# A row-wise log-sum-exp on one core: the logs of the first 51 rows stored in fifteen small pieces between two loads

## The chip, the cores and the metric

The kernel runs on one core of a Trainium2 chip. The metric is the device time in microseconds (us) of one execution. Three runs of the kernel before gave 162.51, 162.53 and 162.57 us, a median of 162.53 us.

## What is computed

The input x is float32 of shape 32 x 512 x 1024; the reduction runs over the last axis, and the output is 32 x 512 float32.

```python
def reference(x, axis):
    x_max = np.max(x, axis=axis, keepdims=True)
    return (x_max.squeeze(axis) + np.log(np.sum(np.exp(x - x_max), axis=axis))).astype(np.float32)
```

The kernel first takes log(sum(exp(x))) without the maximum, in one pass over x, and checks that every sum lies between 1e-18 and 1e18. Only where one does not, a second pass with the maximum runs; with the data of the runs it is skipped.

## The kernel before

**Tiling.** The 16,384 rows of 1024 numbers are spread over 128 partitions, 128 rows to a partition (`x_v`, line 64). Below, "row t" means the t-th row of every partition, 4 KB in each of 128 partitions. The rows go through a ring of 51 row slots in SBUF (`ring`, line 75). `CHUNKS` (line 10) cuts the 128 rows into 17 loads of 4, 15, 16, 16, 16, 14, 13, 9, 7, 5, 4, 3, 2, 1, 1, 1 and 1 rows. They are called load 0 to load 16 here, and the rows of load i are chunk i. So loads 0 to 3 bring the first 51 rows, load 5 has 14 rows, load 6 has 13, load 7 has 9, load 10 has 4 and load 16 is the last row.

**Engines.** All loads and stores are issued by SyncE (SP) in program order, on one DMA queue. `load` (line 135) makes SP wait until VectorE (DVE) or ScalarE (ACT) has finished with the slots that the load overwrites, and then issues one DMA (line 155; line 146 for load 16). ACT takes the exponential of a chunk in place, in one or two pieces (line 235); DVE sums the pieces (line 255, or line 242 row by row). Some rows are summed by ACT itself (line 262, line 225), among them the last four, whose sums go to the PSUM tile `late`.

**Logs.** `take_logs` (line 157) makes ACT wait for the sums of a range of rows and write their logarithm to `res` (line 162). It is called three times: in the turn of chunk 7 (`LN_AT = 7`, line 217) for the 81 rows of chunks 0 to 5, in the turn of the last chunk (line 221) for 43 more rows, and at the end (line 272) for the last four.

**Stores and end.** After all loads, SP waits for the second logs and stores 124 columns of `res` (line 276), then waits for the third and stores the last 4 (line 278). A row of the output is 128 numbers, 512 B, for a partition. Meanwhile DVE compares the sums with the bounds (line 283), TensorE counts the votes (lines 304 and 307), DVE forms the verdict (line 312), and SP, DVE and ACT load it and branch (lines 316 to 321). SP then waits for the other two (line 347), clears the semaphores, and waits for both stores (line 348).

What sets the order around the change is therefore SP's list: a wait there holds back every load behind it.

Of the kernel before, what the change touches and what calls it, by code (L numbers as in the profile page):

```python
# [21 lines left out]
PARTS = ((0, 128, 2), (1, 128, 4), (3, 128, 8), (7, 64, 8), (71, 128, 8))  # L22


LN_AT = 7
LN_LAG = 1


LATE = 4
# [9 lines left out]
def kernel(  # L39
# [6 lines left out]
    nc = tc.nc  # L46
    P = nc.NUM_PARTITIONS
# [17 lines left out]
    out_v = bass.AP(tensor=out.tensor, offset=out.offset, ap=[[NB, P], [1, NB]])  # L65
# [11 lines left out]
    res = nc.alloc_sbuf_tensor("res", [P, NB], fp32).ap()  # L77
# [14 lines left out]
    act_done = nc.alloc_semaphore("act_done")  # L92
# [5 lines left out]
    again = nc.alloc_semaphore("again")  # L98
    act_again = nc.alloc_semaphore("act_again")
    dve_again = nc.alloc_semaphore("dve_again")  # L100
    stored = nc.alloc_semaphore("stored")
    used = sorted(
        sem.num
        for sem in [
            *landed,
            *(act_done, dve_done, pool_done, counted, judged, passed),
            *(again, act_again, dve_again),
        ]
    )
    assert used == list(range(used[0], used[0] + len(used)))  # L110
# [18 lines left out]
    acts = dves = 0  # L129

    def cuts(n, parts):
        ends = [-(-n * k // parts) for k in range(parts + 1)]
        return [(lo, hi) for lo, hi in zip(ends, ends[1:]) if lo < hi]

    def load(i):
        (s, row), r = place[i], CHUNKS[i][0]
        act_wait = max(a for a, _ in busy[s : s + r])
        dve_wait = max(d for _, d in busy[s : s + r])
        if dve_wait:
            nc.sync.wait_ge(dve_done, dve_wait)  # L140
        if act_wait:
            nc.sync.wait_ge(act_done, act_wait)
        dst, src = ring[:, s : s + r], x_v[:, row : row + r]
        if i == len(CHUNKS) - 1:
            for k, (lo, hi) in enumerate(spans):
                nc.sync.dma_start(out=dst[:, :, lo:hi], in_=src[:, :, lo:hi]).then_inc(
                    landed[i + k], 16
                )
        elif i in UNEVEN:
            for first, last, step in PARTS:  # L150
                nc.sync.dma_start(
                    out=dst[first:last:step], in_=src[first:last:step]
                ).then_inc(landed[i], 16)
        else:
            nc.sync.dma_start(out=dst, in_=src).then_inc(landed[i], 16)

    def take_logs(lo, hi, src, dve_wait, act_wait, bias=0.0):
        nonlocal acts
        nc.scalar.wait_ge(act_done, act_wait)
        if dve_wait:  # L160
            nc.scalar.wait_ge(dve_done, dve_wait)
        nc.scalar.activation(out=res[:, lo:hi], in_=src, func=Ln, bias=bias).then_inc(  # L162
            act_done, 1
        )
        acts += 1

    late_row = place[-LATE][1]
    assert not any(n_dve for _, n_dve, _, _ in CHUNKS[-LATE:])

    def total(t):  # L170
        return late[:, t - late_row : t - late_row + 1] if t >= late_row else sums[:, t : t + 1]
# [10 lines left out]
    def pieces(lo, hi):  # L182
        return [(lo + a, lo + b) for a, b in cuts(hi - lo, PIECES)]
# [5 lines left out]
    with nc.body("second_vector", valid_engines=vector):  # L189
        for k, (lo, hi) in enumerate(steps):  # L190
# [5 lines left out]
                out=part, in0=part, in1=peak[:, lo:hi].unsqueeze(2).to_broadcast([P, hi - lo, D])  # L196
# [14 lines left out]
    logged = 0  # L211
    done_before = [(0, 0)]
    for i, (r, n_dve, parts, by_halves) in enumerate(CHUNKS):
        if i:
            load(i)
        s, row = place[i]
        if i == LN_AT:
            logged = place[i - LN_LAG][1]
            take_logs(0, logged, sums[:, :logged], *done_before[i - LN_LAG])
        if i == len(CHUNKS) - 1:  # L220
            take_logs(logged, late_row, sums[:, logged:late_row], *done_before[-LATE])
            early_logs = acts
            for k, (lo, hi) in enumerate(spans):
                nc.scalar.wait_ge(landed[i + k], 16)
                nc.scalar.activation(  # L225
                    out=ring[:, s, lo:hi],
                    in_=ring[:, s, lo:hi],
                    func=Exp,
                    accum_out=late[:, LATE - 1 + k : LATE + k],
                ).then_inc(act_done, 1)  # L230
                acts += 1
            continue
        nc.scalar.wait_ge(landed[i], 16 * (len(PARTS) if i in UNEVEN else 1))
        for lo, hi in cuts(n_dve, parts):
            nc.scalar.activation(  # L235
                out=ring[:, s + lo : s + hi], in_=ring[:, s + lo : s + hi], func=Exp
            ).then_inc(act_done, 1)
            acts += 1
            nc.vector.wait_ge(act_done, acts)
            if by_halves:  # L240
                for j in range(lo, hi):
                    nc.vector.tensor_tensor_reduce(  # L242
                        out=ring[:, s + j, : D // 2],
                        in0=ring[:, s + j, : D // 2],
                        in1=ring[:, s + j, D // 2 :],
                        scale=1.0,
                        scalar=0.0,
                        op0=Alu.add,
                        op1=Alu.add,
                        accum_out=sums[:, row + j : row + j + 1],  # L250
                    ).then_inc(dve_done, 1)
                    dves += 1
                    busy[s + j] = (0, dves)
            else:
                nc.vector.reduce_sum(  # L255
                    out=sums[:, row + lo : row + hi], in_=ring[:, s + lo : s + hi], axis=AX
                ).then_inc(dve_done, 1)
                dves += 1
                for j in range(lo, hi):
                    busy[s + j] = (0, dves)  # L260
        for j in range(n_dve, r):
            nc.scalar.activation(  # L262
                out=ring[:, s + j],
                in_=ring[:, s + j],
                func=Exp,
                accum_out=total(row + j),
            ).then_inc(act_done, 1)
            acts += 1
            busy[s + j] = (acts, 0)
        done_before.append((dves, acts))  # L270
# [2 lines left out]


    nc.sync.wait_ge(act_done, early_logs)
    nc.sync.dma_start(out=out_v[:, :late_row], in_=res[:, :late_row]).then_inc(stored, 16)
    nc.sync.wait_ge(act_done, acts)
    nc.sync.dma_start(out=out_v[:, late_row:], in_=res[:, late_row:]).then_inc(stored, 16)

# [1 line left out]
    def compare(lo, hi, values):  # L281
# [13 lines left out]
        out=ends[:, 1:], in_=sums[:, :late_row], axis=AX, op=Alu.min  # L295
# [26 lines left out]
    with nc.body("second_pass", valid_engines=[*vector, *others]):  # L322
        for k, (lo, hi) in enumerate(steps):
            if k:
                nc.sync.wait_ge(dve_again, 3 * k)
            for a, b in pieces(lo, hi):
                nc.sync.dma_start(
                    out=ring[:, a - lo : b - lo], in_=x_v[:, a:b]
                ).then_inc(again, 16)
        nc.sync.wait_ge(dve_again, 3 * len(steps) + 1)  # L330
        nc.sync.wait_ge(stored, 32)
        nc.sync.dma_start(out=out_v, in_=res).then_inc(stored, 16)
        nc.sync.wait_ge(stored, 48)
        nc.sync.sem_inc(stored, -16)

        for k, (lo, hi) in enumerate(steps):
            part = ring[:, : hi - lo]
            nc.scalar.wait_ge(dve_again, 3 * k + 2)
            nc.scalar.activation(out=part, in_=part, func=Exp).then_inc(act_again, 1)
        nc.scalar.wait_ge(dve_again, 3 * len(steps))  # L340
        nc.scalar.wait_ge(stored, 32)
        nc.scalar.activation(out=res, in_=sums, func=Ln).then_inc(act_again, 1)
        nc.br("last", engines=[*vector, *others])
    nc.switch_bb("last", parent=opening)

    nc.sync.wait_ge(passed, 2)
    nc.sync.sem_clear(range(used[0], used[-1] + 1))
    nc.sync.wait_ge(stored, 32)
# [47 lines left out]
```

## Time and profile before

| | us |
|---|---|
| median of 3 runs | 162.53 |
| the profiled execution | 162.67 |
| its span, first to last instruction | 161.3 |
| around the span in that execution | 1.37 |
| busy in the span: DVE / ACT | 121.9 / 115.1 |
| DMA, share of 16 engines' span | 97.4% |
| DMA packets | 2737, of them 560 under 512 B |

The profile is one execution, recorded by the hardware. Its page gives the busy time of each engine, the DMA activity in 40 slices of the span, the chain of work that ended last, and groups of instructions by source line. The trace behind it also holds when each semaphore was raised by each DMA engine, and a record (start, duration, size) of each DMA packet.

### The profile page before, as it was taken

The numbers are of one execution on the slowest core, as the hardware profiler recorded it, in microseconds if no ns is written. First come the engines' busy times: TensorE is split into PE (matmuls) and PEld (weight loads), VectorE is DVE, ScalarE is ACT, GpSimd is POOL, SyncE is SP. The second block draws the span as 40 slices with busy tenths as digits, with TensorE's granted clock in tenths as the row PEclk, the third lists the DMA queues.
The fourth block names the chain that finished last, engine by engine and source line by source line (L and its number), as shares of the span: only waits on it lengthen the run. The fifth ranks groups of instructions, "written<-read, shape, count | busy, mean of one in ns | idle before, by whom it ended". The sixth has DMA issues, their size and how long they took to land.

```text
span 161.3 us, 149 instructions
## 1 busy us (share of the span) xinstructions
PE 0.2 (0%) x2; PEld 0.1 (0%) x2; DVE 121.9 (76%) x51; ACT 115.1 (71%) x40; POOL 0.4 (0%) x8
## 2 busy tenths in 40 slices
PE   0000000000000000000000000000000000000000
PEld 0000000000000000000000000000000000000000
DVE  0028000003999999999999699999999999999884
ACT  3170005996079960999419993999199999999996
POOL 1000000000000000000000000000000000000000
DMA  7999799979979989989979999999999999999991
GB/s 256 508 488 442 305 472 520 439 341 520 439 341 520 423 358 520 423 358 520 423 325 455 455 455 439 423 423 423 412 402 430 436 420 410 427 436 412 417 407 42
DMA packets 2737, 67.18 MB, mean 417 GB/s; under 512 B 560, under 2 KB 560, under 8 KB 1072
## 3 DMA queue, kind: packets, MB, share of 16 engines
q1 hardware_dynamic: 2736, 67.18, 97.4%
q14 instruction: 1, 0.01, 0.0%
HBM read 67.11 MB, written 0.07 MB: 416 GB/s over the span
## 4 chain that ended last, share of the span: by engine, by line
DMA 49%; DVE 30%; ACT 20%; issue 0%; PE 0%
DMA ring<-in_x_dram 49%; DVE sums L255 29%; ACT ring L235 17%; ACT ring L262 3%; ACT ring L225 1%; ACT res L162 0%; DVE above L283 0%; PE votes L304 0%; DVE verdict L312 0%; PE votes L307 0%
## 5 line engine op out<-in xcount | busy, mean ns | idle before, releaser
L255 DVE TENSOR_REDUCE sums<-ring 128x8 f32<-128x8192 f32 (+5 forms) x14 | 111.2, 7994 | 37.3 <-ACT ring L235 37.2
L235 ACT ACTIVATE ring<-ring 128x8192 f32<-128x8192 f32 (+6 forms) x18 | 104.4, 5836 | 43.9 <-DMA ring<-in_x_dram 43.9
L242 DVE CUSTOM_DVE_ANT_0 ring<-ring 128x512 f32<-128x512 f32 x16 | 9.9, 684 | 0.0
L262 ACT ACTIVATE ring<-ring 128x1024 f32<-128x1024 f32 x8 | 8.2, 1041 | 0.0
L205 ACT ACT_TABLE_LOAD x1 | 1.3, 1283 | 0.8 <-PEq L377 0.8
L262 ACT ACTIVATION_READ_ACCUMULATOR ring<-ring 128x1 f32 x8 | 1.4, 174 | 0.0
L242 DVE DVE_READ_ACCUMULATOR2_ANT sums<- 128x1 f32 x16 | 1.3, 80 | 0.0
L225 ACT ACTIVATE ring<-ring 128x1024 f32<-128x1024 f32 x1 | 1.0, 1040 | 0.0
L283 DVE TENSOR_TENSOR above<-late,bounds 128x8 bf16<-128x8 f32 x1 | 0.2, 168 | 0.7 <-ACT res L162 0.7
L162 ACT ACTIVATE res<-sums 128x81 f32<-128x81 f32 (+1 forms) x2 | 0.5, 248 | 0.0
L312 DVE TENSOR_REDUCE verdict<-votes 1x1 int32<-1x6 f32 x1 | 0.2, 152 | 0.3 <-PE votes L307 0.3
L293 DVE TENSOR_REDUCE ends<-sums 128x1 f32<-128x124 f32 x1 | 0.3, 282 | 0.1
L304 PE MATMUL votes<-above,weights 128*1 128x6 bf16 x1 | 0.2, 167 | 160.0 <-DVE above L283 160.0
L294 DVE TENSOR_REDUCE ends<-sums 128x1 f32<-128x124 f32 x1 | 0.3, 271 | 0.0
L283 DVE TENSOR_TENSOR above<-ends,bounds 128x4 bf16<-128x4 f32 x1 | 0.2, 162 | 0.1
L162 ACT ACTIVATE res<-late 128x4 f32<-128x4 f32 x1 | 0.2, 173 | 0.0
L304 PEld LDWEIGHTS votes<-above,weights 128*1 128x1 bf16 x1 | 0.1, 80 | 160.0 <-DVE above L283 160.0
L307 PE MATMUL votes<-above,weights 128*1 128x6 bf16 x1 | 0.2, 165 | 0.0
L225 ACT ACTIVATION_READ_ACCUMULATOR ring<-ring 128x1 f32 x1 | 0.2, 153 | 0.0
L206 POOL MEMSET bounds<- 128x6 f32 x1 | 0.1, 104 | 0.4 <-POOLq L377 0.4
L207 POOL MEMSET bounds<- 128x6 f32 x1 | 0.1, 104 | 0.0
L377 POOL MEMSET const-bfloat16-1.0<- 128x1 bf16 x1 | 0.1, 103 | 0.0
(6 smaller groups left out, 0.6 us busy)
## 6 DMA issues: line engine op xcount, KB each, us to landing
ring<-in_x_dram SPq DMA_DIRECT2D x1, 7680.0 KB, 25.1
ring<-in_x_dram SPq DMA_DIRECT2D x1, 7168.0 KB, 28.6
ring<-in_x_dram SPq DMA_DIRECT2D x1, 6656.0 KB, 35.7
ring<-in_x_dram SPq DMA_DIRECT2D x1, 4608.0 KB, 20.3
ring<-in_x_dram SPq DMA_DIRECT2D x2, 2048.0 KB, 16.2
ring<-in_x_dram SPq DMA_DIRECT2D x1, 3584.0 KB, 28.5
ring<-in_x_dram SPq DMA_DIRECT2D x1, 2560.0 KB, 27.5
ring<-in_x_dram SPq DMA_DIRECT2D x4, 512.0 KB, 27.2
```

Source lines behind the costliest of these rows:

```text
L162: nc.scalar.activation(out=res[:, lo:hi], in_=src, func=Ln, bias=bias).then_inc(act_done, 1)
L205: nc.scalar.preload_act_table_set("natural_log_exp_and_others")
L225: nc.scalar.activation(out=ring[:, s, lo:hi], in_=ring[:, s, lo:hi], func=Exp, accum_out=late[:, LATE - 1 + k : LATE + k],).then_inc(act_d ...
L235: nc.scalar.activation(out=ring[:, s + lo : s + hi], in_=ring[:, s + lo : s + hi], func=Exp).then_inc(act_done, 1)
L242: nc.vector.tensor_tensor_reduce(out=ring[:, s + j, : D // 2], in0=ring[:, s + j, : D // 2], in1=ring[:, s + j, D // 2 :], scale=1.0, scal ...
L255: nc.vector.reduce_sum(out=sums[:, row + lo : row + hi], in_=ring[:, s + lo : s + hi], axis=AX).then_inc(dve_done, 1)
L262: nc.scalar.activation(out=ring[:, s + j], in_=ring[:, s + j], func=Exp, accum_out=total(row + j),).then_inc(act_done, 1)
L283: nc.vector.tensor_tensor(out=above[:, :, lo:hi], in0=values.unsqueeze(1).to_broadcast([P, 2, hi - lo]), in1=bounds[:, :, lo:hi], op=Alu.i ...
L293: nc.vector.reduce_max(out=ends[:, :1], in_=sums[:, :late_row], axis=AX).then_inc(dve_done, 1)
L294: nc.vector.tensor_reduce(out=ends[:, 1:], in_=sums[:, :late_row], axis=AX, op=Alu.min).then_inc(dve_done, 1)
L304: nc.tensor.matmul(votes[:1, :K], lhsT=weights[:, :1], rhs=above[:, 0], start=True, stop=False)
L307: nc.tensor.matmul(votes[:1, :K], lhsT=weights[:, 1:], rhs=above[:, 1], start=False, stop=True).then_inc(counted, 1)
```

## The change

The first logs are taken in the turn of chunk 5 instead of chunk 7, for the 51 rows of chunks 0 to 3 instead of the 81 of chunks 0 to 5. In the turn of chunk 6, SP, having issued load 6, waits for those logs and stores them: by fifteen DMAs that cover 2, 3, 4, ... 15 and then 9 partitions, 51 numbers (204 B) each. Load 7 is issued behind them. The second logs cover 73 rows instead of 43, and the store behind all loads has 73 columns instead of 124. The fifteen have a semaphore of their own; SP waits for it before the final clearing (and in the second pass, which is skipped).

```diff
-LN_AT = 7
+LN_AT = 5
 LN_LAG = 1
+STORE_AT = 6
+GROUPS = (*range(2, 16), 9)
...
+    stored_early = nc.alloc_semaphore("stored_early")
...
         if i == LN_AT:
             logged = place[i - LN_LAG][1]
             take_logs(0, logged, sums[:, :logged], *done_before[i - LN_LAG])
+            first_logs, first_logged = acts, logged
+        if i == STORE_AT:
+            nc.sync.wait_ge(act_done, first_logs)
+            for k, n in enumerate(GROUPS):
+                p = sum(GROUPS[:k])
+                nc.sync.dma_start(
+                    out=out_v[p : p + n, :first_logged], in_=res[p : p + n, :first_logged]
+                ).then_inc(stored_early, 16)
+            assert sum(GROUPS) == P
...
     nc.sync.wait_ge(act_done, early_logs)
-    nc.sync.dma_start(out=out_v[:, :late_row], in_=res[:, :late_row]).then_inc(stored, 16)
+    nc.sync.dma_start(
+        out=out_v[:, first_logged:late_row], in_=res[:, first_logged:late_row]
+    ).then_inc(stored, 16)
...
+    nc.sync.wait_ge(stored_early, 16 * len(GROUPS))
     nc.sync.wait_ge(passed, 2)
     nc.sync.sem_clear(range(used[0], used[-1] + 1))
     nc.sync.wait_ge(stored, 32)
```

## The prediction, made before the changed kernel was run

> **What bounds the kernel now.** I read the page's DMA lines first. The second line gives GB/s in the 40 slices.
>
> ```profile
> DMA  7999799979979989989979999999999999999991
> GB/s 256 508 488 442 305 472 520 439 341 520 439 341 520 423 358 520 423 358 520 423 325 455 455 455 439 423 423 423 412 402 430 436 420 410 427 436 412 417 407 42
> DMA packets 2737, 67.18 MB, mean 417 GB/s; under 512 B 560, under 2 KB 560, under 8 KB 1072
> q1 hardware_dynamic: 2736, 67.18, 97.4%
> ```
>
> The DMA engines work from the second slice to the next to last. The dips stand where large loads meet and are an effect of when 64 KB packets are counted, for the landings leave no hole: the three loads of 16 rows landed at 45.20, 64.56 and 83.91 us, 19.36 apart; the loads of one row end 1.28 us apart. A line through these is 1.205 us a row and 0.075 us a load, and every load in between lies on it. Then the chain that ended last, in order of time (start, length, what):
>
> ```profile
> 122.29 24.89 DMA ring<-in_x_dram
> 147.17 0.02 issue
> 147.19 2.76 ACT ring L235
> ...
> 155.45 3.01 ACT ring L262 x6
> 158.46 0.01 ACT res L162
> 158.47 0.03 issue
> 158.49 1.11 ACT ring L225 x2
> 159.60 0.02 issue
> 159.62 0.18 ACT res L162
> ```
>
> From load 10's landing (147.17) ACT works without a gap. Load 16 landed at 158.42 and its exponential began at 158.49, behind a log, so ACT is late by about 0.05 us there: DMA stream and ACT are level at the end. What delays load 10 delays the end by as much; an earlier stream gains at most 0.2 us, since ACT was free only 0.23 us before 147.19. The last store was issued at 159.82 and landed at 161.23; SP's last instruction began at 161.27. The waits of SP's queue (us, times, longest) and the two stores (KB, us to landing):
>
> ```profile
> SPq L155 <- DVE sums L255: 122.8, 7, 52.7
> SPq L276 <- ACT res L162: 28.1, 1, 28.1
> ...
> SPq L278 <- ACT res L162: 0.8, 1, 0.8
> ```
>
> ```profile
> out_dram<-res SPq DMA_DIRECT2D x1, 62.0 KB, 2.2
> ...
> out_dram<-res SPq DMA_DIRECT2D x1, 2.0 KB, 1.4
> ```
>
> SP mostly waits for DVE. The first store, issued at 158.61, landed at 160.85, 0.38 us ahead of the second: its size does not set the end.
>
> Last, the packet records. A 128-row DMA makes 128 data packets and 16 semaphore packets of 4 B (19 DMAs x 16 = 304; with the stores' 256 these are the 560 under 512 B). The 16 engines run side by side with equal work and keep a constant lag: load 6's semaphore packets started from 115.302 to 116.218, and load 16's from 157.187 to 158.002. A load has landed when the last engine's has.
>
> **The change, part by part.**
>
> *The first logs move* from 81 rows at 128.09 us to 51 rows in chunk 5's turn. The timeline there:
>
> ```profile
> 96.93 1.04 ACT L262 ACTIVATE ring<-ring 128x1024 f32<-128x1024 f32 x1
> 97.88 0.19 ACT L262 ACTIVATION_READ_ACCUMULATOR ring<-ring 128x1 f32 x1
> 100.88 12.24 ACT L235 ACTIVATE ring<-ring 128x7168 f32<-128x7168 f32 x2 [2.81 <-DMA ring<-in_x_dram]
> ```
>
> ACT would take this log at 98.07, about 0.24 us (the row of 43 columns is 238 ns, that of 81 is 257). The sums it waits for are done at 89.43, when DVE's first run of five reductions ends. The idle 2.81 us before load 5 hide it; without them it would cost 0.24. The 0.16 us freed before 128.25 are worth nothing: ACT finds load 8 (136.22) and load 10 still to come.
>
> *The second logs grow* from 43 to 73 columns on the path at 158.35. By the two rows, 19 ns for 38 columns, 30 more cost **0.015 us**.
>
> *SP's list gains a wait and fifteen issues* ahead of load 7 and all behind it. The wait ends at about 98.3, and SP has nothing to do until DVE frees load 7's slots (issue at 107.23). An issue lasts 0.33 to 0.72 us in the trace and back to back 0.48 from start to start, so fifteen take 7.2 us and end at 105.5. They would delay the issue from 0.59 us each on. Even at the longest, 0.72, it comes at 109.1, with the engines on load 6 until 115.3 or later; from issue to first packet is 0.85 us (158.61 to 159.457), so 5 us of cover are left. Cost: nothing; once that cover is gone, every further us counts in full.
>
> *The DMA engines* get 128 packets of 204 B and the fifteen stores' semaphore packets between loads 6 and 7. Packets that write to the output followed each other on one engine after 6 ns (16 B) and 23.5 ns (496 B); by size 204 B gives 13. A semaphore packet lasts 9, and behind one the next load's first packet began after 5. So a store costs an engine that takes part 22 ns at most. No store here has fewer than 128 rows, so the trace does not show which engines take part. The bounds for the engine that lands last are nothing (it has no part) and 15 x 22 = **0.33 us**. A row is one packet in every record, so a store of n under 16 rows leaves 16 - n engines without data. If all groups start at the same engine, the sixteen get 15, 15, 14, 13, 12, 11, 10, 9, 8, 6, 5, 4, 3, 2, 1 and 0 rows; the engines that are ahead at that point are ahead by 0.92, 0.86, 0.82, 0.76, 0.75, 0.70, 0.60 and so on to 0. If these two orders agree, every engine can take 57 ns a store before it becomes the last. I take **0**, as fifteen of the sixteen have a lead and 22 ns uses at most 0.33 of it, and keep 0.33 as the other end. Below nothing: the last engine's packets from 116 us on are together 0.39 us over the shortest of their size, so disturbed phases could give back at most that, of which ACT lets 0.2 through.
>
> The Trainium skill bears on this ("DMA: Bandwidth & Descriptors", section "Why a DMA increments its semaphore by 16 and not by 1"): a DMA from SP uses the largest number of engines, up to 16, that divides its row counts, from the lowest-numbered on, and only these write the semaphore. By it the sixteenth engine has no packet at all and the term is 0 if that engine is the last; no run here shows it so far, nor the engines' order.
>
> *The last stores.* 292 B for 496 shortens eight packets an engine by some 7 ns each, 0.06 us, off the path. On SP one semaphore wait is added ahead of the clearing, which began at 161.129 and took 81 ns; with the step to the next instruction it already ends level with the last landing. The wait row lasts 17 ns and SP's gap between instructions is 0.05: between 0 and 0.07, and I take **0.05**.
>
> *Sum:* 0.015 + 0 + 0.05 = +0.065 us on the profiled span of 161.29, so 161.35, and 162.73 with the 1.37 around it (162.67 before). The runs' median was 0.14 below this execution: 162.53 + 0.065 = **162.6 us**.
>
> **Rivals.**
>
> *The last engine pays.* If the stores go round the engines in turn, each gets 8 rows with 8 to 15 semaphores, 0.18 to 0.24 us; if the last engine has the row of every store, 0.33. With the 0.065 this is +0.24 to +0.40: **162.8 to 162.9**. For it: the trace does not order the engines. Against: one group in fifteen only has 15 rows.
>
> *A semaphore behind a write to the output holds its engine.* The stores' semaphore packets (first at 159.645) took effect 0.36 us later (160.008). If the next packet had to wait that long, an engine with fifteen stores would lose 5.4 us, 4.5 beyond its lead of 0.92, and load 7 and all later ones would come so much later: **167.1 us**, slower. It decides from 57 ns a store. Against it: behind a load's semaphore packet the next load began 5 ns later, though that too took 0.44 us to take effect (115.302 to 115.746). For it: those packets follow writes to SBUF, and nothing was queued behind a store's; the case is not in the trace. The skill's same page ("Anatomy of one DMA") says that the semaphore waits for the write's receipt and that this is longest with HBM, yet calls the bubble about one cycle; by the first alone 167 follows, by the second none.
>
> *The stream runs smoother.* With less lead the engines meet in other phases and the last one loses fewer of its 0.39 us: 0.2 gained, **162.4**; little in the profile supports it.
>
> *It doesn't do what it says:* the fifteen stores would be late if the log were, but its sums are 8.6 us early.
>
> **How the numbers follow.** Forecast 0.53, own range 162.5 to 162.7. Last engine pays 0.20, half of it beyond 0.2%. Held engine 0.21, of which 0.05 with holds short enough to stay under 163.2. Smoother 0.06, of which 0.04 beyond 0.2% below for what I can't name. So slower by over 0.2% (0.33 us, about what a measurement of this kernel can tell from no change) has 0.10 + 0.21 = 0.31, faster 0.04, within 0.65. The range takes in the forecast, the paying engine, the short holds and the smoother stream's 162.4: 162.35 to 163.2. Outside are the long holds (0.16) and the unnamed gain (0.04).
>
> **What would show it.** Right: the first log near 98.1 in an idle stretch; fifteen store issues from 98.3 to about 105.5; load 7 issued near 107.2; load 6 landed at 116.6 and load 7 still at 127.5, 10.95 later; the last engine's packet chain without small packets between the two loads; the span near 161.35. Wrong: load 7 landing 0.2 to 0.4 late (the last engine pays), or several us late with gaps behind the small semaphore packets (held), an issue of load 7 past 115, or an instruction fetch that falls on the last engine in mid-stream (one of 8 KB took 0.61 us at 159.5).

## The result, and the profile after

The changed kernel took 164.06 us (median of four runs, 163.73 to 164.19) where the kernel before took 162.52 (four runs, 162.23 to 162.57): a ratio of 1.0095, 95% interval 1.0075 to 1.0115. It is slower by about 1.5 us; 162.6 had been forecast, and 164.06 lies outside the range of 162.35 to 163.2. The profiled execution took 163.97 us with a span of 162.6, 1.30 us more than the profiled one of before.

The page's DMA lines of the changed kernel:

```profile
span 162.6 us, 165 instructions
...
DMA  7999979959969979998999989999999999999990
...
DMA packets 2993, 67.18 MB, mean 413 GB/s; under 512 B 816, under 2 KB 816, under 8 KB 1328
...
q1 hardware_dynamic: 2992, 67.18, 97.0%
```

There are 256 more small packets: 128 rows and 128 semaphores. So the fifteen stores together write 128 semaphore packets and not 15 x 16 = 240. The engines are busy as before, for 1.3 us longer.

The chain that ended last (start, length, what):

```profile
122.05 26.34 DMA ring<-in_x_dram
148.39 0.02 issue
148.41 2.76 ACT ring L248
...
156.68 3.01 ACT ring L275 x6
159.69 0.06 issue
159.75 1.11 ACT ring L238 x2
160.86 0.02 issue
160.88 0.18 ACT res L166
```

Load 10 is issued 0.24 us earlier than before and still lands 1.22 us later (148.39 against 147.17). Everything behind follows it, so the loss is in the stream of loads. SP and ACT around the stores, from the timeline:

```profile
96.59 1.04 ACT L275 ACTIVATE ring<-ring 128x1024 f32<-128x1024 f32 x1
97.63 0.23 ACT L166 ACTIVATE res<-sums 128x51 f32<-128x51 f32 x1
97.88 5.47 SPq L229 DMA_DIRECT2D out_dram<-res  x15
100.67 12.24 ACT L248 ACTIVATE ring<-ring 128x7168 f32<-128x7168 f32 x2 [2.81 <-DMA ring<-in_x_dram]
106.89 22.90 SPq L159 DMA_DIRECT2D ring<-in_x_dram  x9
...
128.91 7.03 ACT L248 ACTIVATE ring<-ring 128x8192 f32<-128x8192 f32 x1 [0.76 <-DMA ring<-in_x_dram]
```

The log lies in ACT's idle gap, the fifteen issues end at 103.35, and load 7 is issued at 106.89, when DVE frees its slots. Nothing is late on SP. But ACT now waits 0.76 us for load 7, which it found landed in the kernel before:

```profile
128.25 7.01 ACT L235 ACTIVATE ring<-ring 128x8192 f32<-128x8192 f32 x1
```

Load 6 landed at 116.55 us (116.59 before), load 7 at 128.89 (127.53 before): **1.36 us late**.

Bytes moved between the two landings, by stretches (the last two columns are the DMA share and GB/s; a packet counts in full where it starts), before:

```profile
116.00:118.00 2.00, 0.00 (x0) 0.00 (x0) 2.00 (x1) 1.39 (x1) 0.00 (x0) 1.00 0.86 369
118.00:120.00 2.00, 0.00 (x0) 0.00 (x0) 2.00 (x1) 2.00 (x1) 0.00 (x0) 1.00 1.18 498
```

and after:

```profile
116.00:118.00 2.00, 0.00 (x0) 0.00 (x0) 2.00 (x1) 1.43 (x1) 0.00 (x0) 1.00 0.93 334
118.00:120.00 2.00, 0.00 (x0) 0.00 (x0) 2.00 (x1) 2.00 (x1) 0.00 (x0) 1.00 0.85 369
```

From 116 to 120 us packets of 1.41 MB are started instead of 1.73: the engines are at work, but on packets that are late to end. The packet records say which. They do not name the engine, and neither do the records of when a semaphore was raised; but each packet starts where another ends, so they fall into sixteen chains, one for each engine. The small packets of a chain are counted between load 6's semaphore packet and the first of its eight load 7 packets (36,864 B):

```
stores on   load 6's      first packet of load 7:
the engine  semaphore at  start      lasted, ns
15          115.584       115.872    2904
15          115.740       116.028    2922
14          115.783       116.052    2728
13          115.561       115.811    2656
12          115.784       116.016    2576
11          115.494       115.707    2556
10          115.731       115.925    2398
 9          115.424       115.600    2265
 8          115.982       116.138    1755
 6          115.760       115.878    1413
 5 to 0     115.851 to    115.932 to 1364 each
            116.236       116.261
```

The counts follow from the time between the two starts, at 19 ns a store: 15, 15, 14 and so on to 0 stores, a row and a semaphore packet each. The small packets are cheap. The cost is in the packet behind them. It lasts 1364 ns on engines with up to five stores, as it did on all engines before (one 1366), and up to 2922 ns on one with fifteen. The second engine of the table accounts for the loss: 0.29 us of small packets and 1.56 of hold, from 115.740, end at 118.950; the last engine of before, from 116.224, ended that packet at 117.588. The difference is the 1.36 us.

So the question for the experiments was what holds that packet: the rows, their destination, or the semaphores.

### The profile page after: what moved, and what is told of

Same layout as the page of the kernel before. It is cut to its first block, busy times and chain, and to the rows that moved or that the text cites. A ratio compares the mean times of both kernels' runs of the same rounds, so it can differ in the third digit from the quotient of the medians.

```text
span 162.6 us, 165 instructions
## 1 busy us (share of the span) xinstructions
PE 0.2 (0%) x2; PEld 0.1 (0%) x2; DVE 122.0 (75%) x51; ACT 115.3 (71%) x40; POOL 0.4 (0%) x8
## 4 chain that ended last, share of the span: by engine, by line
DMA 49%; DVE 29%; ACT 20%; issue 0%; PE 0%
DMA ring<-in_x_dram 49%; DVE sums L268 29%; ACT ring L248 17%; ACT ring L275 2%; ACT ring L238 1%; ACT res L166 0%; DVE above L298 0%; PE votes L319 0%; DVE verdict L327 0%; PE votes L322 0%
## 5 line engine op out<-in xcount | busy, mean ns | idle before, releaser
L166 ACT ACTIVATE res<-sums 128x51 f32<-128x51 f32 (+1 forms) x2 | 0.5, 246 | 0.0
```

## The experiments

All are edits of the changed kernel, timed in the same rounds as the kernel before; ratios are to that kernel, with 95% intervals. Each still computes the whole output. "Hold" is the time by which a packet exceeds the shortest of its size.

**One early store.** Eight rows on each engine, one semaphore.

```diff
-GROUPS = (*range(2, 16), 9)
+GROUPS = (128,)
```

> The 51 columns are stored early by one DMA of 128 partitions: 8 rows and 1 semaphore packet on each of 16 engines, in place of 0 to 15 rows with 0 to 15 semaphores. Theory A (each store's semaphore holds its engine until the write to the output in front of it is received, some 0.18 us one after the other, of which the first large packet behind hides about 1.3 us): no packet of load 7 held, every engine later by 8 x 13 ns + 6 = 0.11 us, time about 162.5 + 0.11 + 0.065 = 162.7 us. Theory B (each small row written to the output costs its engine time, about 0.1 us, and the semaphores nothing): the 36,864 B packet is held as behind 8 rows in the changed kernel, 0.39 us, now on all engines and so on the last one: about 163.1 us. Theory C (any semaphore costs, wherever the data goes): as A.

Measured: 162.64 us against 162.57, ratio 1.0011 (1.0002 to 1.0020). All sixteen engines had 8 rows, and every first packet of load 7 lasted 1364 ns. From load 6's semaphore to load 7's first packet it was 0.115 us. Theory B, the rows, falls: eight rows cost what their packets last and hold nothing.

**Eight early stores of 16 partitions.** The same rows on each engine, eight semaphores.

```diff
-GROUPS = (*range(2, 16), 9)
+GROUPS = (16,) * 8
```

> The same bytes by eight DMAs of 16 partitions: again 8 rows on each engine, but 8 semaphore packets in place of 1. Theory A: the hold of 8 stores in the changed kernel, 0.39 us, on every engine, the last included, and 8 x 19 ns of packets, 0.15: 162.5 + 0.39 + 0.15 + 0.065 = 163.1 us. Theory B: the same as the one store of 128 partitions, whatever that is. Theory C: as A.

Measured: 163.12 us, 1.0047 (1.0034 to 1.0060), as theories A and C had it. All sixteen first packets are held, 0.28 to 0.83 us. Between this kernel and the last one only the number of DMAs, and with it of semaphores, differs. No run has a DMA without its semaphore, so "a semaphore" below stands for a small DMA with the semaphore behind it.

**The fifteen into SBUF.**

```diff
+    aside = nc.alloc_sbuf_tensor("aside", [P, 51], fp32).ap()
...
-                    out=out_v[p : p + n, :first_logged], in_=res[p : p + n, :first_logged]
+                    out=aside[p : p + n], in_=res[p : p + n, :first_logged]
...
-        out=out_v[:, first_logged:late_row], in_=res[:, first_logged:late_row]
+        out=out_v[:, :late_row], in_=res[:, :late_row]
```

> The fifteen small DMAs go to a spare SBUF tile instead of the output; all 124 columns are stored at the end as before. Same issues, rows and semaphores on the same engines. Theories A and B, both of which need the output in HBM: no packet of load 7 held; the packets alone, 0.29 us on the engine with fifteen, are mostly within its lead: 162.55 to 162.8 us. Theory C: held as in the changed kernel, about 164 us.

Measured: 164.03 us, 1.0090 (1.0077 to 1.0103), as the changed kernel. The first packets behind fifteen stores lasted 3012 and 3075 ns, those behind up to four 1364. My theory A falls in the part that named the output: a semaphore behind a write to SBUF holds as long. Theory C stands.

**The logs moved, nothing stored early.** The loop over `GROUPS` and its waits are left out, and the store at the end has 124 columns.

> The logs are split 51 and 73 as in the changed kernel, but nothing is stored early: one store of 124 columns at the end, no added wait. All theories: the stream of loads as before, 162.5 to 162.6 us. If it is later than that by over 0.2 us, the logs or the last store have a part in the loss.

Measured: 162.51 us against 162.57, 1.0006 (0.9995 to 1.0018): no difference. The logs have no part in the loss.

From the holds I then wrote theory D. On one engine the semaphores take effect one after the other. The held packets end some 3.2 us after the first small packet with fifteen stores, and some 1.95 us after it with eight; from this I estimated 0.6 us for the first semaphore and about 0.19 for each further one. Meanwhile the engine works on at the load behind, up to a limit.

**The same fifteen at four places.**

```diff
-GROUPS = (*range(2, 16), 9)
+GROUPS = (15, 14, 13, 12, 11, 10, 9, 9, 8, 7, 6, 5, 4, 3, 2)
+AT = {6: (0, 6), 7: (6, 10), 8: (10, 13), 9: (13, 15)}
...
-        if i == STORE_AT:
-            nc.sync.wait_ge(act_done, first_logs)
-            for k, n in enumerate(GROUPS):
+        if i in AT:
+            if i == STORE_AT:
+                nc.sync.wait_ge(act_done, first_logs)
+            for k in range(*AT[i]):
+                n = GROUPS[k]
```

> The same fifteen stores, to the output, with the same sizes and so the same rows and semaphores in total on each engine, but at four places of the queue: six behind load 6, four behind load 7, three behind load 8, two behind load 9. Theory D (now: each semaphore packet takes its turn some 0.19 us after the one before on its engine, wherever the data went, the first after 0.6 us; the first large packet behind moves its data meanwhile but cannot end before the last of them, so k stores at one place cost 0.6 + 0.19 (k - 1) less the time of that packet and of the small ones): the holds are 0.06, 0.03, 0.16 and 0.14 us on the engines with all of them, mostly inside their lead: 162.6 to 162.8 us. Theory E (the cost goes by the number of small stores on an engine, wherever they stand in the stream): as the changed kernel, about 164 us.

Measured: 162.69 us, 1.0010 (1.0001 to 1.0020). The same stores on the same engines lose 0.16 us instead of 1.5. Theory E, the number alone, falls; what counts is how many stand in a row. Six in a row held the packet behind by 0.10 to 0.46 us, somewhat more than the 0.06 worked out, and most of it lay in the leads.

**Four early stores of 32 partitions.**

```diff
-GROUPS = (*range(2, 16), 9)
+GROUPS = (32,) * 4
```

> Four early stores of 32 partitions: 8 rows on each engine as with one store of 128 or eight of 16, with 4 semaphores. Theory D: 0.6 + 3 x 0.19 = 1.17 us is covered by the packet of 1.36 behind, so no hold; small packets 8 x 13 + 4 x 6 = 0.13 us: about 162.65 to 162.75 us, level with the one store. Were each semaphore paid without cover (0.55 us for 8 of them, 0.07 each): about 162.85 to 162.9 us.

Measured: 162.64 us, 1.0008 (0.9998 to 1.0017). Fourteen of the sixteen first packets lasted 1364 ns, one 1404 and one 1442. Four in a row are free, as one is; eight are not.

**Eight stores from ACT's queue.** Issued by ACT behind the log, in the turn of chunk 5.

```diff
-STORE_AT = 6
-GROUPS = (*range(2, 16), 9)
+STORE_AT = 5
+GROUPS = (16,) * 8
...
-            nc.sync.wait_ge(act_done, first_logs)
+            nc.scalar.wait_ge(act_done, first_logs)
...
-                nc.sync.dma_start(
+                nc.scalar.dma_start(
```

> The eight stores of 16 partitions issued by ACT, on its own DMA queue, right behind the log in its idle gap before load 5, in place of SP; they no longer stand in a row between loads 6 and 7 but come about 0.35 us apart while packets of loads 5 and 6 of 2 us are under way. Theory D: at most a few semaphores meet behind one large packet and hide under the next one, so no hold remains: 162.6 to 162.8 us, against 163.12 from SP's queue. If the hold goes with the stores whatever is queued around them: 163.1 us.

Measured: 162.82 us, 1.0013 (1.0002 to 1.0024), and load 7 landed at 127.47 us. From ACT's queue the rows are taken one at a time among the packets of loads 5, 6 and 7, from 101.59 to 125.23 us, so that none follows another at once on its engine, and they hold nothing: no packet of load 7 lasts over 1365 ns. They cost ACT instead, since an issue takes it 0.47 us (SP took 0.46 for the same eight): chunk 5's exponential starts 1.2 us after load 5 landed (100.69 us), "issue" being what it waited for.

```profile
98.12 3.74 ACTq L229 DMA_DIRECT2D out_dram<-res  x8
101.90 12.24 ACT L248 ACTIVATE ring<-ring 128x7168 f32<-128x7168 f32 x2 [3.82 <-issue]
```

**Thirty in a row into SBUF.** The fifteen sizes twice, into two spare tiles; all 124 columns are stored at the end. This one did not test what it was made for.

```diff
-            for k, n in enumerate(GROUPS):
-                p = sum(GROUPS[:k])
+            for k, n in enumerate(GROUPS * 2):
+                p = sum(GROUPS[: k % len(GROUPS)])
...
-                    out=out_v[p : p + n, :first_logged], in_=res[p : p + n, :first_logged]
+                    out=aside[k // len(GROUPS)][p : p + n], in_=res[p : p + n, :first_logged]
```

> Thirty DMAs at the one place, the fifteen sizes twice, into two spare SBUF tiles; 124 columns stored at the end as before. Theory D: 15 more semaphores in a row on the first engines, 15 x 0.19 = 2.85 us more than the fifteen to SBUF (164.03): about 166.9 us. Were the loss instead a single disturbance that fifteen stores already fill (one receipt, one switch of direction): about 164 to 164.5 us.

Measured: 169.96 us, 1.0459 (1.0441 to 1.0476), far over either number. SP's timeline says why:

```profile
80.64 0.33 SPq L160 DMA_DIRECT2D ring<-in_x_dram  x1
98.23 22.77 SPq L230 DMA_DIRECT2D aside<-res  x30
121.05 9.03 SPq L160 DMA_DIRECT2D ring<-in_x_dram  x9
```

A small DMA from SBUF to SBUF takes SP 0.76 us to issue, where one to the output took 0.36 (5.47 us for fifteen). Load 7 is issued at 121.05, after load 6 has landed at 116.64, and the engines stand idle. Almost nothing starts to move in between, 4 GB/s from 116 to 118 us:

```profile
116.00:118.00 2.00, 0.00 (x0) 0.00 (x0) 2.00 (x1) 1.33 (x1) 0.00 (x0) 1.00 0.03 4
```

So this shows another thing: what the issues cost once SP's cover is gone. Load 7 landed at 134.77, 7.2 us late. In the run with fifteen into SBUF load 7 was issued at 109.59, still in cover.

**Thirty in a row to the output.** The dose again, with issues that stay in cover.

```diff
-GROUPS = (*range(2, 16), 9)
+GROUPS = (4,) * 22 + (5,) * 8
```

> Thirty early stores to the output at the one place, twenty-two of 4 partitions and eight of 5: 128 rows as before, now 30 rows and 30 semaphores on each of four engines, 8 on a fifth, none on the rest. SP issues them in about 10 us, load 7 some 1 us later than before, with the engines on load 6 until 115. Theory D: the last of 30 semaphores 0.6 + 29 x 0.19 = 6.1 us after the first small packet, less 0.57 for the small packets and 1.36 for the large one: those engines held 4.2 us, with 0.57 of packets and a lead of about 0.8: 162.55 + 3.95 + 0.065 = 166.5 us. If the loss went by rows or bytes (the same 128 rows and 26 KB): about 164 us or less.

Measured: 166.71 us against 162.47, 1.0260 (1.0245 to 1.0275). SP is in time, ACT waits:

```profile
98.15 10.31 SPq L229 DMA_DIRECT2D out_dram<-res  x30
108.50 21.45 SPq L159 DMA_DIRECT2D ring<-in_x_dram  x9
...
131.43 7.03 ACT L248 ACTIVATE ring<-ring 128x8192 f32<-128x8192 f32 x1 [3.33 <-DMA ring<-in_x_dram]
```

The same 128 rows and 26 KB, on four engines, lose 4.2 us instead of 1.5. On those four the first packet of load 7 lasted 4544 to 4729 ns, on the fifth, with eight stores, 2040; the engines without stores kept to 1364 to 1371. This run also shows the semaphores one by one. With four engines alike, the stores' semaphore is raised in groups of four, each within 15 to 27 ns; from 118.72 to 121.26 us fifteen such groups follow each other every 0.18 us. The four held packets end at 121.43, one such step behind the last group. Four raisings within 15 ns also speak against the semaphore itself as what is slow, though no run gave the stores of a kernel more than one. The sum came out close, but not by the expected parts: the hold was 3.2 to 3.4 us and not 4.2 (so 0.16 us a semaphore on average, by theory D's sum), and the lead of 0.8 was not there, since these engines began their stores at 116.13 to 116.31, among the last to end load 6.

**Eight of 16 ahead of a smaller packet.**

```diff
-STORE_AT = 6
-GROUPS = (*range(2, 16), 9)
+STORE_AT = 9
+GROUPS = (16,) * 8
```

> The eight stores of 16 partitions behind load 9 instead of load 6, so that the first packet behind them is one of load 10, 16,384 B or 0.61 us, instead of 36,864 B or 1.36 us. Theory D with a cover of one packet: 0.6 + 7 x 0.19 = 1.93 us, less 0.15 and 0.61: a hold of 1.17 us on every engine and 0.15 of packets: about 163.9 us, against 163.12 behind load 6. If the cover is a fixed time or several packets: about 163.1 us.

Measured: 163.13 us, 1.0036 (1.0024 to 1.0048), the same as behind load 6. Theory D falls in one part: the cover is not one packet. The first four packets of load 10 on four engines (start, ns; the shortest of 16,384 B lasts 611):

```
141.220  654   141.870  622   142.489 1321   143.807  611
141.242  676   141.915  620   142.532 1182   143.710  611
141.390  704   142.090  620   142.707 1241   143.944  611
141.577  638   142.212  622   142.830  964   143.790  611
```

The hold falls on the third packet, on all sixteen engines (964 to 1373 ns). An engine works on for some 1.3 us, or 33 to 37 KB (two packets of 16,384 B pass, one of 36,864 does not), behind the small packets, and then stops until the semaphores have caught up. Which of the two sets the limit, time or bytes, these runs do not separate, as both go together at an engine's rate.

## Why the prediction was wrong, point by point

- **The step that failed is "The DMA engines".** The change was priced by how long small packets last, "a store costs an engine that takes part 22 ns at most", with 0.33 us as the far end. The packets cost that (19 ns). What the step left out is that the semaphores take effect one by one, about 0.18 us apart, and that an engine runs only some 1.3 us ahead of them: it priced a semaphore by its packet of 9 ns and the 5 ns to the next start, and put the wait behind it at nothing. Fifteen in a row held the engine by 1.56 us beside 0.29 of packets. The step's own mark, 57 ns a store before an engine becomes the last, was useful: the fifteen cost (1.56 + 0.29) / 15 = 0.12 us each, over it.
- **The rival "a semaphore behind a write to the output holds its engine" had the mechanism, and was given 0.21.** Three of its parts were off. The price was 0.36 us a semaphore, taken from one semaphore alone (159.645 to 160.008); in a row they follow at about half of that. It has nothing to do with the output (the run with fifteen into SBUF). And it knew no cover, so 1.3 us went missing. These made 167.1 out of what was 164.06. The evidence against it, a load's packet that starts 5 ns behind a semaphore, was a start: the start of a packet does not say when it can end, and a single semaphore is covered, as the run with one store shows.
- **Which engines take part:** the 15, 15, 14 ... 0 that was assumed is what the chains of packets show. The Trainium skill states the rule that leads to these counts ("DMA: Bandwidth & Descriptors", section "Why a DMA increments its semaphore by 16 and not by 1"): a DMA from SP runs on the largest number of engines, up to 16, that divides its row counts, from the lowest-numbered on. The counts agree; the numbers of the engines no trace here shows. The same section of the Trainium skill says that SP itself writes the rest of the sixteen at once. Fifteen early raisings of that semaphore, from 98.34 to 103.53 us, one an issue, agree.
- **"The last engine pays"** did not happen: the engine that ended load 6 last had one store, and one with fifteen became the last by its hold.
- **The leads** were smaller than assumed for the first engines: 0.65 and 0.50 us for the two with fifteen stores, not 0.92 and 0.86. In the run with thirty stores there was none on the engines that needed it. An order of the engines is not something to build on here.
- **"The stream runs smoother"** was there in part. Behind the first packet of load 7 an engine lost, on average, 0.21 us over the shortest packets, and 0.43 before; load 16 landed 1.22 us late where load 7 had been 1.36.
- **SP's list** was right in that nothing was late; the issues came 0.36 us apart, not 0.48, and ended at 103.35, and load 7 was issued at 106.89. **The first logs** were right: 0.23 us in the gap of 2.81.
- **The last logs and stores** were near in size: the step from the log's start to the exponential's grew from 0.144 to 0.170 us (0.015 expected), and the added wait and the clearing put SP's last instruction 0.10 us behind the last landing instead of 0.04 (0.05 expected). The last store still lands alone at the end.

One reading of the prediction was too smooth: not every load lies on the line of 1.205 us a row and 0.075 a load. Load 8, with seven rows, took 8.69 us where the line gives 8.51. Nothing in the sum used it.

From load 16's landing to the end of the span it is 2.97 us, 2.87 before. So the span's 1.32 us are 1.22 of stream and 0.10 of tail. The medians differ by 1.54; the 1.30 between the two profiled executions lies within the interval of the ratio.

**What stays open** is why a semaphore takes about 0.18 us behind another. It does not matter whether the row in front goes to the output or to SBUF, and eight rows in front of one semaphore hold nothing; what each semaphore waits for was not told apart. The Trainium skill ("DMA: Bandwidth & Descriptors", section "Anatomy of one DMA — SWDGE (gpsimd) path") calls the bubble of a semaphore write about one cycle; the section follows a DMA issued by GpSimd, and those here come from SP. One semaphore behind a load, with the next start 5 ns later, does not speak against it; for fifteen in a row the measurement decides against it.

No version was faster than the kernel before. The end did not wait for the store that was shortened, and the best early stores from SP, one DMA of 128 partitions and four of 32, came within about 0.1% of it (1.0011 and 1.0008).

## What to carry to other kernels

Between two loads of a stream that bounds the kernel, count the semaphores that stand in a row on one DMA engine, not the bytes. Here one DMA of 128 partitions in front of a large load cost 0.1 us, four of 32 the same, eight of 16 cost 0.5, and fifteen small ones that put up to fifteen on one engine cost 1.5, for the same 26 KB. Where small transfers must share a queue with a stream that bounds the kernel, put a few between each two large loads rather than all at one place. And look at how long the packets behind last, since those in front show nothing.

## What the runs showed of the hardware

- Semaphores of one engine that follow small writes take effect about 0.18 us apart (thirty on each of four engines: groups of four every 0.18 us from 118.72 to 121.26), while the packets themselves start 19 ns apart. The other runs fit, but do not tell the engines apart: 128 semaphores, eight an engine, were spread over 1.69 us, and with up to fifteen an engine over 2.76.
- A DMA engine starts packets of the next load at once and carries on for some 1.3 us; only then does a packet wait. The hold shows on the first packet where it is 36,864 B and on the third where they are 16,384 B.
- SP needs about twice as long to issue a small DMA from SBUF to SBUF as one of the same sizes to the output: 0.76 against 0.36 us. To the output it took 0.34 us for 4 or 5 partitions and 0.46 for 16; ACT took 0.47 for 16.
